# The first SwiGLU of the second layer: its first block of columns in seven half-width products

## The chip, the cores and the metric

The kernel runs on one core of a Trainium2 chip. The metric is the device time of one execution in microseconds (us); the time before is the median of three runs. The traces come from the hardware profiler: one profiled execution, with the start and the length of the instructions on each engine. TensorE (PE in the rows) multiplies and writes PSUM, VectorE (DVE) and ScalarE (ACT) work elementwise, GpSimd (POOL) hardly works here, and SyncE (SP) issues the weight transfers.

## The reference

Two layers work on 512 tokens of width 1024 in float32. Each layer is

```
h = h + 1/2 * SwiGLU_1(RMSNorm(h))      # w_gu 1024 x 5632, w_down 2816 x 1024
h = h + mixer(RMSNorm(h))               # short convolution, attention, gates
h = h + 1/2 * SwiGLU_2(RMSNorm(h))
h = h + sigmoid(RMSNorm(h) @ W_pg) * (p[i] @ W_pp)     # "ple"
swiglu(x) = (silu(g) * u) @ w_down, with g, u the halves of x @ w_gu
```

and a last RMSNorm follows. The change is in the `x @ w_gu` of SwiGLU_1 of the second layer, and in the place of the sum of squares of its RMSNorm.

## The kernel before

**Layout.** Everything is held transposed: `h` is eight tiles of 128 features x 512 tokens. A name in the rows begins with its stage: `a0`, `m0`, `b0`, `e0` are SwiGLU_1, mixer, SwiGLU_2 and ple of the first layer, `a1`, `m1`, `b1`, `e1` those of the second. The stage ahead of `a1` is `e0`.

**Precision.** Each float32 operand is held as two parts, `h` (the rounded value, cast on ScalarE, line 70 for weights and 205 or 208 for activations) and `l` (the rest, subtracted on VectorE, lines 71, 206, 209), and each product is three matmuls, `h*h`, `h*l`, `l*h` (lines 213 to 215, and 451). Weights come by DMA in halves of 128 x 1024 (`st`, 10 buffers) and are split into `wh` and `wl` (4 buffers each).

**Two ways to multiply.** `projs` takes whole columns: 128 output features x 512 tokens. `Sevens` takes a block of 2 x 2 quarters (two halves of the 1024 inputs, two halves of the block's columns) and two halves of the tokens, and makes seven half-width products of 24 matmuls with 256 tokens in place of eight (Strassen's scheme). `Quad` makes the sums of weight quarters on VectorE (lines 142, 147, 150, 153). `Halved` makes the sums of activations: `own(j)` takes row `j` of the lower half of the features (line 393), `other(j)` joins it with row `j+4` (lines 408 to 411) and casts the results `t` and `u`. Product 1 needs rows 0 to 3 of the input alone, product 5 `t` of the lower rows, product 2 rows 4 to 7, products 6, 3, 7 and 4 the joined sums. `step(n, j)` is product `j` of block `n`.

**The norm.** `normed` splits each row of `h` times its gain (`x`), and adds the squares of the rows up one by one in `acc` (line 283). `rms` turns `acc`'s two parts (`ah`, `al`) into sums over the features by two matmuls with ones (`ps`, lines 292 and 293) and takes the reciprocal root `r`, with which results are scaled later.

**What `early` selects.** In `ffn`, `n_whole` is the number of pairs of columns (g and u of 128 features) that are taken whole. It is 4 for the first stage, 2 with `early=2`, and 0 with `early=3`:

```
n_whole = 4 if first else 0 if early > 2 else 2
```

With 2, the first pair is taken whole, then come the two matmuls of the sums, then the second pair, then block 1 in sevens. With 0, block 0 is in sevens as well and the start is

```
            x_ins, sums = ys.other(KD // 2 - 1, xs)

            with tc.issue_after(x_ins):
                step(0, 1)
                step(0, 5)
            r = rms(acc, D, name)
            with tc.issue_after(x_ins):
                step(1, 1)
                step(1, 5)
            order = (2, 6, 3)
```

so that the two matmuls of the sums stand behind two products. `early_rows` makes the rows of `Halved` while the rows of `h` come in: with 2 it makes whole rows 0 and 1 there and the others behind the first columns; with 3 it makes `own` of rows 0 to 3 and `other` of rows 0 to 2, and splits the weights of three products ahead (lines 506 to 514).

**What orders the work.** Instructions are put in order when the program is built, by a scheduler that `issue_after` steers; each engine then has a fixed list. The second SwiGLUs (`b0`, `b1`) use `early=3` already, behind the mixer; `a1` uses 2, behind `e0`. In `e0` each row of `h` is made by `ple_add`: line 963 (VectorE, from the gate's columns), line 965 (sigmoid on ScalarE), lines 969 and 970 on VectorE, where the last is the add to `h`. In the mixer a row of `h` takes one add (line 883).

Of the kernel before, what the change touches and what calls it, by code (L numbers as in the profile page):

```python
# [173 lines left out]
def trunk_kernel(ctx, tc, dims, x, p, positions, gains, rope_c, weights, out):  # L174
# [860 lines left out]
                    dma.dma_start(out=out[row:row + P, kk * 512:(kk + 1) * 512], in_=o)  # L1035

    for l in range(DEPTH):
        ffn(l, "ffn1", f"a{l}", l == 0, rotary if l == 0 else None, 2 if l else 0)
        mixer(l)
        ffn(l, "ffn2", f"b{l}", early=3)  # L1040
        ple(l, l == DEPTH - 1)
# [47 lines left out]
```

## Time and profile before

| | us |
|---|---|
| median of 3 runs (2280.04 to 2280.17) | 2280.16 |
| the profiled execution | 2279.72 |
| its span in the trace | 2277.7 |
| PE busy | 2269.1 |
| DVE busy | 1817.2 |
| ACT busy | 1170.5 |
| mean granted TensorE clock | 0.999 |

A span is the time from the first to the last instruction in the trace. Busy time counts a matmul to its modelled end, so matmuls that follow one another overlap; the distance of two starts tells what one costs in a row. The rows of a timeline give start, length, engine, line and names, and in brackets the idle time of the engine just ahead and what ended it.

### The profile page before, as it was taken

What the parts mean: (1) busy time and instruction counts of PE and PEld (TensorE: products, weight loads), DVE (VectorE), ACT (ScalarE), POOL (GpSimd) and SP (SyncE); (2) the same over time, 40 slices, a digit from 0 to 9 for tenths busy, and PEclk for the clock granted to TensorE, in tenths of its full rate; (3) what the DMA queues carried; (4) which work ended last, traced back from release to release, by engine and by line L of the source; (5) the groups of instructions that cost most, each with busy time, mean ns of one, the idle gap of its engine ahead of it and who ended that gap; (6) DMA issues with size and microseconds to landing.
All of it is one profiled execution on the core that took longest, in us unless ns stands there. A gap on an engine that the chain in (4) does not pass through costs nothing.

```text
span 2277.7 us, 35049 instructions
## 1 busy us (share of the span) xinstructions
PE 2269.1 (100%) x14320; PEld 2063.7 (91%) x14320; DVE 1817.2 (80%) x2540; ACT 1170.5 (51%) x1770; POOL 38.1 (2%) x42
## 2 busy tenths in 40 slices
PE   9999999999999999999999999999999999999998
PEld 8999988899888999998899999888999889999988
DVE  8878778877867988877798887768878689877865
ACT  7444445456745644444664444445567365444455
POOL 0000000000200000000000000000001000000000
PEclk9999999999999999999999999999999999999999
DMA  5333343134121333334223333322331214323321
GB/s 195 113 109 101 104 125 104 55 111 130 47 66 56 110 111 105 102 111 130 83 84 96 109 99 115 121 88 70 112 120 38 74 39 138 111 93 102 112 84 38
DMA packets 63088, 222.77 MB, mean 98 GB/s; under 512 B 7248, under 2 KB 7248, under 8 KB 62928
## 3 DMA queue, kind: packets, MB, share of 16 engines
q1 hardware_dynamic: 62352, 219.76, 30.9%
q8 instruction: 112, 1.84, 0.3%
q10 hardware_dynamic: 576, 0.79, 0.1%
q14 instruction: 48, 0.39, 0.1%
HBM read 218.42 MB, written 2.10 MB: 97 GB/s over the span
## 4 chain that ended last, share of the span: by engine, by line
PE 98%; DVE 1%; ACT 0%; DMA 0%; issue 0%; SPq 0%; ACTq 0%
PE b0pd L213 2%; PE b1pd L213 2%; PE a1pd L213 2%; PE a0pd L213 2%; PE b1pd L214 2%; PE a1pd L214 2%; PE a0pd L214 2%; PE b0pd L214 2%; PE a0pd L215 2%; PE b0pd L215 2%; PE a1pd L215 2%; PE b1pd L215 2%; PE e1gp L213 1%; PE e1gp L215 1%; PE e1gp L214 1%; PE m1mop L213 1%
## 5 line engine op out<-in xcount | busy, mean ns | idle before, releaser
L70 ACT CAST wh<-st 128x1024 fp32r<-128x1024 f32 (+1 forms) x457 | 476.6, 1046 | 564.2 <-issue 64.4
L71 DVE TENSOR_TENSOR wl<-st,wh 128x1024 fp32r<-128x1024 f32 (+1 forms) x458 | 554.7, 1213 | 153.5 <-ACT wh L70 152.9
L70 ACT CAST wh<-s 128x1024 fp32r<-128x1024 f32 x98 | 103.1, 1053 | 132.4 <-DVE s L147 8.9
L71 DVE TENSOR_TENSOR wl<-s,wh 128x1024 fp32r<-128x1024 f32 x98 | 119.4, 1219 | 13.5 <-ACT wh L70 13.4
L150 DVE TENSOR_TENSOR st<-st,s 128x1024 f32<-128x1024 f32 x49 | 60.0, 1224 | 1.2
L147 DVE TENSOR_TENSOR s<-s,st 128x1024 f32<-128x1024 f32 x49 | 59.8, 1220 | 0.2
L142 DVE TENSOR_TENSOR s<-st,st 128x1024 f32<-128x1024 f32 x49 | 59.8, 1220 | 0.1
L153 DVE TENSOR_TENSOR st<-st,st 128x1024 f32<-128x1024 f32 x49 | 59.7, 1219 | 0.1
L559 DVE SCALAR_TENSOR_TENSOR h<-b1pd,h 128x512 f32<-128x512 f32 x40 | 27.6, 689 | 9.0 <-PE b1pd L215 9.0
L559 DVE SCALAR_TENSOR_TENSOR h<-b0pd,h 128x512 f32<-128x512 f32 x40 | 27.6, 689 | 9.0 <-PE b0pd L215 9.0
L559 DVE SCALAR_TENSOR_TENSOR h<-a1pd,h 128x512 f32<-128x512 f32 x40 | 27.6, 689 | 7.6 <-PE a1pd L215 7.5
L559 DVE SCALAR_TENSOR_TENSOR h<-a0pd,h 128x512 f32<-128x512 f32 x40 | 27.5, 688 | 6.4 <-PE a0pd L215 6.3
L107 POOL MEMSET wh<- 128x256 f32 x4 | 1.1, 314 | 1188.9 <-DVE wl L71 1188.9
L296 ACT ACT_TABLE_LOAD x8 | 10.3, 1283 | 0.1
L878 DVE TENSOR_TENSOR m1g<-m1mop,m1g 128x512 f32<-128x512 f32 x8 | 5.5, 690 | 5.9 <-PE m1mop L215 5.9
L878 DVE TENSOR_TENSOR m0g<-m0mop,m0g 128x512 f32<-128x512 f32 x8 | 5.5, 690 | 5.5 <-PE m0mop L215 5.5
L989 ACT ACTIVATE fsq<-h 128x256 f32<-128x256 f32 (+1 forms) x10 | 4.8, 481 | 9.9 <-DVE h L970 9.9
L299 DVE SCALAR_TENSOR_TENSOR e1t<-e1t,e1ms 128x512 f32<-128x512 f32 x1 | 0.7, 696 | 8.5 <-ACT e1ms L298 8.5
L117 DVE TENSOR_TENSOR kl<-st,kh 128x512 fp32r<-128x512 f32 x10 | 6.8, 685 | 0.5 <-ACT kh L116 0.5
L705 DVE TENSOR_TENSOR m1g<-m1cop,m1g 128x512 f32<-128x512 f32 x8 | 5.5, 688 | 2.0 <-PE m1cop L215 2.0
L705 DVE TENSOR_TENSOR m0g<-m0cop,m0g 128x512 f32<-128x512 f32 x8 | 5.5, 687 | 2.0 <-PE m0cop L215 2.0
L676 DVE TENSOR_TENSOR m0z<-m0Vp,m0c 128x512 f32<-128x512 f32 x4 | 2.8, 692 | 5.1 <-PE m0Vp L215 5.1
(11283 smaller groups left out, 8847.7 us busy)
## 6 DMA issues: line engine op xcount, KB each, us to landing
st<-in_weights SPq DMA_DIRECT2D x406, 512.0 KB, 3.6
h<-in_x SPq DMA_DIRECT2D x8, 256.0 KB, 5.4
st<-in_weights SPq DMA_DIRECT2D x7, 256.0 KB, 5.2
out<-fo SPq DMA_DIRECT2D x7, 256.0 KB, 2.3
e0pi<-in_p SPq DMA_DIRECT2D x2, 256.0 KB, 3.7
e1pi<-in_p SPq DMA_DIRECT2D x2, 256.0 KB, 3.8
st<-in_weights ACTq DMA_DIRECT2D x1, 256.0 KB, 3.2
pos_i<-in_positions ACTq DMA_DIRECT2D x1, 256.0 KB, 3.9
```

The lines of the kernel that those rows point to most:

```text
L70: self.nc.scalar.copy(hi[:, w], src[:, w])
L71: last = self.nc.vector.tensor_tensor(lo[:, w], src[:, w], hi[:, w].bitcast(F32), ALU.subtract)
L142: tt(self.s, self.a21, self.a22, ALU.add)
L147: tt(self.s, self.s, self.a11, ALU.subtract)
L150: tt(self.a12, self.a12, self.s, ALU.subtract)
L153: tt(self.a11, self.a11, self.a21, ALU.subtract)
L213: nc.tensor.matmul(ps, wh, vh, start=first, stop=False)
L214: nc.tensor.matmul(ps, wh, vl, start=False, stop=False)
L215: nc.tensor.matmul(ps, wl, vh, start=False, stop=last)
L559: nc.vector.scalar_tensor_tensor(h[m], ps, 0.5, h[m], ALU.mult, ALU.add)
L705: nc.vector.tensor_tensor(gates[m], ps, gates[m], ALU.mult)
L878: nc.vector.tensor_tensor(t, mla_ps[m], t, ALU.mult)
```

## The change

`a1` takes its start in the form that the second SwiGLUs have: `early` is 3 for the second layer's first SwiGLU, which makes `n_whole` 0. The diff is one line:

```
-        ffn(l, "ffn1", f"a{l}", l == 0, rotary if l == 0 else None, 2 if l else 0)
+        ffn(l, "ffn1", f"a{l}", l == 0, rotary if l == 0 else None, 3 if l else 0)
```

Block 0 of `w_gu` (two pairs of columns, 96 matmuls of 512 tokens) becomes seven products (168 matmuls of 256 tokens); the other blocks and `w_down` stay. The order of the instructions shows where the sums stand now.

On VectorE before, from the add that finishes the last row of `h` in `e0` (`h_96`) to the second part of the sum of squares (`a1al`); rows 4 to 6 of the norm were split ahead of these:

```order
L970 TENSOR_TENSOR h_96<-h_96,e0g_11231 128x512
L71 TENSOR_TENSOR wl_11439<-st_11436,wh_11438 128x1024
L283 TENSOR_TENSOR a1acc<-a1acc,a1sq 128x512
L209 SCALAR_TENSOR_TENSOR a1x7l<-h_96,cols,a1x7h 128x512
L283 TENSOR_TENSOR a1acc<-a1acc,a1sq 128x512
L142 TENSOR_TENSOR s<-st_11698,st_11700 128x1024
L206 TENSOR_TENSOR a1al<-a1acc,a1ah 128x512
```

On VectorE of the changed kernel, from the same add, through row 5 of the norm with its joined sums, to the beginning of row 6:

```order
L970 TENSOR_TENSOR h_96<-h_96,e0g_11231 128x512
L209 SCALAR_TENSOR_TENSOR a1x5l<-h_94,cols,a1x5h 128x512
L283 TENSOR_TENSOR a1acc<-a1acc,a1sq 128x512
L409 TENSOR_TENSOR a1t_11258<-a1y_11321,a1x_11257 128x256
L410 TENSOR_TENSOR a1u_11322<-a1t_11258,a1x_11257 128x256
L206 TENSOR_TENSOR a1t1l<-a1t_11258,a1t1h 128x256
L411 TENSOR_TENSOR a1u_11322<-a1y_11321,a1u_11322 128x256
L206 TENSOR_TENSOR a1u1l<-a1u_11322,a1u1h 128x512
L209 SCALAR_TENSOR_TENSOR a1x6l<-h_95,cols,a1x6h 128x512
```

Row 6 takes the same seven instructions, and the list goes on from its last one:

```order
L206 TENSOR_TENSOR a1u2l<-a1u_11341,a1u2h 128x512
L209 SCALAR_TENSOR_TENSOR a1x7l<-h_96,cols,a1x7h 128x512
L283 TENSOR_TENSOR a1acc<-a1acc,a1sq 128x512
L206 TENSOR_TENSOR a1al<-a1acc,a1ah 128x512
L409 TENSOR_TENSOR a1t_11288<-a1y_11393,a1x_11287 128x256
```

So 16 instructions stand between the two rows that enclosed five before. On TensorE of the changed kernel the two matmuls of the sums (`a1ps`) stand between product 5 of block 0 (`a10c`) and product 1 of block 1 (`a11b`):

```order
L451 MATMUL a10c<-a1t3h,wh_11366 128x256
L451 MATMUL a10c<-a1t3l,wh_11366 128x256
L451 MATMUL a10c<-a1t3h,wl_11367 128x256
L292 MATMUL a1ps<-a1ah,ones 128x512
L293 MATMUL a1ps<-a1al,ones 128x512
L451 MATMUL a11b<-a1x0h,wh_11378 128x256
```

That is behind 48 matmuls of 256 tokens; before they stood behind 48 matmuls of 512 tokens.

## Rows read from the trace of the kernel before

**Rows 1.** Part 1 of the page: busy us, share of the span, instructions.

```profile
PE 2269.1 (100%) x14320; PEld 2063.7 (91%) x14320; DVE 1817.2 (80%) x2540; ACT 1170.5 (51%) x1770; POOL 38.1 (2%) x42
```

**Rows 2.** All waits of PE: us in total, times, longest us.

```profile
PE idle L321 <- DVE hpi L251: 1.0, 1, 1.0
PE fss L1001 <- DVE fsq L982: 0.8, 1, 0.8
PE a0pg L231 <- ACT a0x0h L208: 0.2, 1, 0.2
```

**Rows 3.** The chain from 1125 to 1185: start us, us, what.

```profile
1135.03 0.23 PE a1pg L213
...
1145.91 0.24 PE a1ps L292
...
1157.29 2.87 PE a11b L451 x24
1160.16 2.88 PE a11a L451 x24
```

**Rows 4.** The timeline of PE where b1 begins.

```profile
1864.69 0.28 PE L451 MATMUL b10b<-b1x0h,wh 128*128 128x256 f32 x1
...
1867.56 0.28 PE L451 MATMUL b10c<-b1t0h,wh 128*128 128x256 f32 x1
...
1870.44 0.40 PE L292 MATMUL b1ps<-b1ah,ones 128*128 128x512 f32 x1
...
1870.91 0.28 PE L451 MATMUL b11b<-b1x0h,wh 128*128 128x256 f32 x1
```

**Rows 5.** The timeline of DVE where b1 begins.

```profile
1864.89 0.69 DVE L883 TENSOR_TENSOR h<-m1wop,h 128x512 f32<-128x512 f32 x1
1865.50 0.41 DVE L206 TENSOR_TENSOR b1t2l<-b1t,b1t2h 128x256 fp32r<-128x256 f32 x1
1865.83 0.69 DVE L206 TENSOR_TENSOR b1u2l<-b1u,b1u2h 128x512 fp32r<-128x512 f32 x1
1866.44 0.75 DVE L209 SCALAR_TENSOR_TENSOR b1x7l<-h,cols,b1x7h 128x512 fp32r<-128x512 f32 x1
1867.11 0.69 DVE L283 TENSOR_TENSOR b1acc<-b1acc,b1sq 128x512 f32<-128x512 f32 x1
1868.48 0.69 DVE L206 TENSOR_TENSOR b1al<-b1acc,b1ah 128x512 fp32r<-128x512 f32 x1 [0.69 <-ACT b1ah L205]
1869.11 0.43 DVE L409 TENSOR_TENSOR b1t<-b1y,b1x 128x256 f32<-128x256 f32 x1
1869.57 0.42 DVE L410 TENSOR_TENSOR b1u<-b1t,b1x 128x256 f32<-128x256 f32 x1
```

**Rows 6.** The timeline of ACT where b1 begins.

```profile
1867.83 0.62 ACT L205 CAST b1ah<-b1acc 128x512 fp32r<-128x512 f32 x1 [0.90 <-DVE b1acc L283]
...
1871.82 1.28 ACT L296 ACT_TABLE_LOAD   x1
```

**Rows 7.** The timeline of DVE where a1 begins.

```profile
1133.71 0.69 DVE L963 TENSOR_TENSOR e0g<-e0gp,e0r 128x512 f32<-128x512 f32 x1
...
1136.78 0.69 DVE L970 TENSOR_TENSOR h<-h,e0g 128x512 f32<-128x512 f32 x1
1137.38 1.22 DVE L71 TENSOR_TENSOR wl<-st,wh 128x1024 fp32r<-128x1024 f32 x1
1138.52 0.69 DVE L283 TENSOR_TENSOR a1acc<-a1acc,a1sq 128x512 f32<-128x512 f32 x1
...
1141.94 0.69 DVE L206 TENSOR_TENSOR a1al<-a1acc,a1ah 128x512 fp32r<-128x512 f32 x1 [0.33 <-ACT a1ah L205]
```

**Rows 8.** The same stretch of ACT.

```profile
1140.33 1.06 ACT L70 CAST wh<-st 128x1024 fp32r<-128x1024 f32 x1 [1.58 <-issue]
```

**Rows 9.** Stretches at the end: us, busy PE, PEld, DVE, ACT, POOL; then granted clock, DMA.

```profile
2271.00:2272.00 1.00, 0.32 (x3) 0.08 (x2) 0.55 (x4) 0.26 (x1) 0.00 (x0) 1.00 0.00 0
...
2274.00:2275.00 1.00, 0.00 (x0) 0.00 (x0) 0.00 (x0) 0.00 (x0) 0.00 (x0) 0.50 1.00 371
```

## The prediction

> **What bounds the kernel now.** I read the engines' shares first: TensorE is busy 2269.1 of 2277.7 us, VectorE 80%, ScalarE 51% [rows 1]. Then TensorE's waits: there are three in the whole trace, 2.0 us together, two where the kernel begins and one where it ends [rows 2]. So there is no idle time of TensorE around `a1` to win, and none to hide anything in: a matmul saved shortens the time by its own cost, and a wait that the change adds is paid in full, since TensorE has no later wait that could shrink by it.
>
> What one matmul costs is read from the distance of starts. The chain runs through `a1`'s two whole pairs from 1135.03 to 1157.29 [rows 3]: 22.26 us for 98 matmuls of 512 tokens, the 96 of the two pairs and the two of the sums: 0.227 each. A half-width product of 24 matmuls with 256 tokens takes 2.88 [rows 3], 0.120 each: a matmul of half the width costs 53% of a full one.
>
> The third view is the order of the two engines where such a start exists already. In `b1`, product 1 begins at 1864.69, product 5 at 1867.56, the sums at 1870.44 and the next product at 1870.91 [rows 4]: back to back, with no wait. But VectorE finished `b1al` only at 1868.48 + 0.69 = 1869.17 [rows 5]. So in `b1` the sums were ready 1.3 us ahead of their use. `a1` gets that start behind another stage, and the question is whether its sums come in time as well.
>
> **The change part by part.**
>
> *TensorE's work.* Removed: 96 matmuls x 0.227 = 21.8 us. Added: 7 products x 2.88 = 20.2. The gain is 1.6 us, 0.07%. The halves of weights are as many as before, and their transfers too.
>
> *Elementwise work.* Block 0 now needs seven splits of weights in place of four and four sums of quarters, each as long as a split, 1.22 us [rows 7]; VectorE has room for them over the stage, so by themselves I cost them at nothing, as long as they do not stand ahead of something that TensorE waits for. They do, at the start, and that is the rest of this part.
>
> *When TensorE wants the sums.* What precedes `a1` on TensorE is unchanged, so product 1 begins at 1135.03 [rows 3], and `a1ps` is wanted two products on: 1135.03 + 5.76 = 1140.79. Before, it stood 48 full matmuls behind, at 1145.91 [rows 3], and `a1al` was done at 1141.94 + 0.69 = 1142.6 [rows 7], with 3.3 us to spare. It would have been 1.8 us late already for the new place.
>
> *When VectorE delivers them.* The add that makes the last row of `h` stood at 1136.78 [rows 7]. It can't come earlier than the end of `e0`'s matmuls at 1135.03 and two instructions of 0.60 on the way, 1136.3; I take 1136.8 and keep 1136.3 to 1137.8 (one 1.14 us split later). Before, five instructions lay between this add and `a1al`. Now there are 16, in the order shown above: rows 5 and 6 of the norm, each with its joined sums, and row 7. Their cost by distance of starts: line 209 0.67, line 283 0.60 [rows 5, 7], lines 409 and 410 0.46 each, the split of a half row (line 206) 0.33 [rows 5], line 411 followed by the cast of `u` on ScalarE and back. That way there and back is seen between `b1acc` and `b1al`: 1868.48 - 1867.11 = 1.37 behind an add of 0.69, with VectorE idle for 0.69 of it [rows 5], the cast being 0.62 [rows 6]; behind an add of 0.42 it is 0.27 shorter, 1.10. In `b1` other work stood between, here nothing does. Then the split of `u`, 0.60. One row: 0.67 + 0.60 + 0.46 + 0.46 + 0.33 + 1.10 + 0.60 = 4.2 us.
>
> So `a1al` starts at 1136.8 + 0.60 + 2 x 4.2 + 0.67 + 1.37 = 1147.8 and ends at 1148.5. TensorE, which has run the first matmul of the sums on `a1ah` just ahead, waits with the second: 1148.5 - 1140.79 - 0.23 = **7.5 us**. Behind it in TensorE's list stands everything else, product 1 of block 1 first, although its weights are ready by then. With the bounds of `h` this is 7.0 to 8.5.
>
> VectorE keeps its order: at 1141.94 `a1al` had made it wait for 0.33 [rows 7], while the split behind it, whose cast on ScalarE was over at 1140.33 + 1.06 = 1141.39 [rows 8], stayed where it was. The Trainium skill (TensorE: Matmul & The Clock Gate, the table at its head, row on queue depth) states that VectorE and ScalarE take their queues strictly first in, first out; by that rule rows 5 and 6 can't be overtaken, and the trace agrees; if an engine could overtake, the sum would be -1.6.
>
> *What is late next.* TensorE goes on at 1148.75 and wants product 2 of block 0 two products later, at 1154.5. Its weights' second part stands on VectorE behind: row 7's joined sums (0.46 + 0.46 + 0.34), a split of weights (1.14) and of a half row (0.33), which ends at 1151.2 counted from 1148.4; the split of `u`, whose cast stands on ScalarE behind the table load of 1.28 [rows 6] and the first step of the root, so at about 1152.0; then two sums of quarters, 1.14 each, a step of the root, and the split itself, 1.22: 1156.8. The product's third matmul wants it at about 1154.7, so some 2 us are lost; I take **1.8**, between 0 and 2.5. VectorE is busy 80% over the kernel [rows 1], so a lag of 7 us shrinks by a fifth of the time that passes; when block 2's first weights are wanted, some 30 us on, about 1 us of it is left, which I count as **1.1**, between 0 and 2.
>
> *The clock.* At the end of the kernel TensorE's last matmuls lie between 2271 and 2272 at a granted clock of 1.00, and from 2274 on it is 0.50, the 1.2 GHz level [rows 9]: the clock falls soon behind the work. A wait of 7.5 us will very likely do the same, and product 1 of block 1 then runs at half the rate, 2.88 us longer if it stays so for a whole product. How long it stays low no row shows. The first 2.9 us lost in this way cost nothing more, since they take the place of the 1.8 and 1.1 above, which VectorE's list sets and not TensorE; each further product at the low level costs 2.88. I take no more than that, and keep two further ones, 5.8, as the other end. The Trainium skill (the same page, Part 1: The HAM clock gate) states that the throttled clock is the default and activity releases it. By it a stall costs more than its length; the sum by rows has that already up to one product.
>
> *Sum.* -1.6 + 7.5 + 1.8 + 1.1 = +8.8 us. Against the profiled execution, 2279.72, that is 2288.5; the median of the runs stands 0.44 above it, so **2289.0 us**, 0.39% slower.
>
> **The rivals.**
>
> *The sums come in time.* `b1` speaks for it: same start, no wait, and there `b1al` began 3.6 us after the last add to `h` [rows 5]. Against it: there four instructions lay between, of rows 6 and 7 alone, and here the list is 16 long and in sequence. It decides at 1140.3: if `a1al` starts by then, TensorE goes on without a stop and the change gives its -1.6, 2278.6 us. That takes 7.5 us off the walk above.
>
> *The waits half as long.* If VectorE reached rows 5 and 6 well ahead of the add to `h`, the wait would be one row shorter, some 3.3, and nothing late behind it: -1.6 + 3.3 = +1.7, 2281.9. Against it: the list is fixed and the add stands ahead of them.
>
> *The clock stays low.* The wait as forecast, then three products at the low level: 8.8 + 5.8 = +14.6, 2294.8; with two, 2291.9. For it: no row shows the clock rise again once it has fallen [rows 9]. Against it: the products behind the wait follow one another without a gap, but for 2.9 us in all.
>
> **How the numbers follow.** The forecast, with its bounds (7.0 to 8.5 for the first wait, 0 to 4.5 for the others together, -1.6): +5.4 to +11.4, 2285.6 to 2291.6; I give it 0.74. The clock low for two products or more: 0.13. Half as long: 0.05. In time: 0.07. Something that wins more than the counted 1.6: 0.01. A range of 2286.3 to 2292.2 leaves out the low ends, the sums in time and a long low clock. About 0.2%, 4.6 us, is what a measurement of this kernel can tell from no change. Slower: 0.74 and 0.13 and a little of the half case, 0.88. Same: the rest of that, and the sums in time, 0.11. Faster: 0.01.
>
> **What the profile after would show.** Right: among TensorE's waits one at `a1ps` of 7 to 8 us, released by VectorE at `a1al`; `a1al` some 11 us behind the last add to `h` of `e0`; smaller waits or a granted clock of 0.50 in the 10 us behind; seven products of 2.88 in place of 21.8 us, seen in the distance from `a1`'s first matmul to `b1`'s. Wrong: `a1ps` following product 5 without a gap, a wait released by a DMA, or a first product of `a1` that itself starts late because VectorE's longer list held up `e0`.

## The result and the profile after

The changed kernel takes 2290.51 us (median of 6 runs, 2289.66 to 2290.65), the kernel before 2280.16 (6 runs, 2280.04 to 2280.53): a ratio of 1.0045 [1.0034, 1.0055], 10.35 us slower. The forecast was +8.8, 2289.0, with a range of 2286.3 to 2292.2. The profiled execution of the changed kernel took 2290.54 with a span of 2288.4 us.

Part 1 of the page after, beside [rows 1]: TensorE is busy 2.7 us longer, although its work is 1.6 us less.

```profile
PE 2271.8 (99%) x14392; PEld 2069.5 (90%) x14392; DVE 1827.9 (80%) x2556; ACT 1173.2 (51%) x1782; POOL 38.1 (2%) x42
```

All waits of TensorE after, beside [rows 2]: two are new, one at the sums and one at `a12c`, product 5 of block 2.

```profile
PE a1ps L292 <- ACT a1ah L205: 7.3, 1, 7.3
PE idle L321 <- DVE hpi L251: 1.0, 1, 1.0
PE fss L1001 <- DVE fsq L982: 0.8, 1, 0.8
PE a12c L451 <- ACT wh L70: 0.8, 1, 0.8
```

TensorE's timeline after: first matmul of `a1`, the two of the sums, then the first of products 1 and 5 of block 1, of product 2 of block 0 and its third, and the first of block 3.

```profile
1135.67 0.28 PE L451 MATMUL a10b<-a1x0h,wh 128*128 128x256 f32 x1
...
1148.85 0.80 PE L292 MATMUL a1ps<-a1ah,ones 128*128 128x512 f32 x1 [7.26 <-ACT a1ah L205]
1149.57 0.79 PE L293 MATMUL a1ps<-a1al,ones 128*128 128x512 f32 x1
1150.16 0.42 PE L451 MATMUL a11b<-a1x0h,wh 128*128 128x256 f32 x1
...
1154.56 0.28 PE L451 MATMUL a11c<-a1t0h,wh 128*128 128x256 f32 x1
...
1157.44 0.28 PE L451 MATMUL a10a<-a1x4h,wh 128*128 128x256 f32 x1
...
1158.08 0.39 PE L451 MATMUL a10a<-a1x4h,wl 128*128 128x256 f32 x1
...
1202.32 0.28 PE L451 MATMUL a13b<-a1x0h,wh 128*128 128x256 f32 x1
```

The same two ends in TensorE's timeline of the kernel before:

```profile
1134.87 0.39 PE L213 MATMUL a1pg<-a1x0h,wh 128*128 128x512 f32 x1
...
1191.68 0.28 PE L451 MATMUL a13b<-a1x0h,wh 128*128 128x256 f32 x1
```

From the first matmul of `a1` to the first of block 3 is thus 1191.68 - 1134.87 = 56.81 us before and 66.65 after. **The stage is 9.84 longer**, and it adds up from starts alone:

| part of the stage | us |
|---|---|
| 168 half-width matmuls (20.16) for 96 whole ones (21.79) | -1.6 |
| the sums begin at 1148.85, two products (5.76) behind 1135.67 would be 1141.43 | +7.42 |
| the two matmuls of the sums, 1148.85 to 1150.16, before 0.46; the second begins only when `a1al` is done | +0.85 |
| product 1 of block 1, 1150.16 to 1154.56 = 4.40 in place of 2.88 | +1.52 |
| products 2, 6 and 3 of block 0 from 1157.44 | +0.29 |
| three products across block 2's start, 10.03 in place of 8.64 | +1.39 |

Of the 10.82 between the two profiled executions 0.80 more lies ahead of `a1` and 0.2 behind block 3.

VectorE's timeline after, beside [rows 7], from the last add to `h` to the second part of the sums and to the weights of product 2 of block 0:

```profile
1137.57 0.68 DVE L970 TENSOR_TENSOR h<-h,e0g 128x512 f32<-128x512 f32 x1
1138.17 0.74 DVE L209 SCALAR_TENSOR_TENSOR a1x5l<-h,cols,a1x5h 128x512 fp32r<-128x512 f32 x1
...
1142.45 0.75 DVE L209 SCALAR_TENSOR_TENSOR a1x6l<-h,cols,a1x6h 128x512 fp32r<-128x512 f32 x1
...
1146.73 0.75 DVE L209 SCALAR_TENSOR_TENSOR a1x7l<-h,cols,a1x7h 128x512 fp32r<-128x512 f32 x1
1147.40 0.68 DVE L283 TENSOR_TENSOR a1acc<-a1acc,a1sq 128x512 f32<-128x512 f32 x1
1148.83 0.69 DVE L206 TENSOR_TENSOR a1al<-a1acc,a1ah 128x512 fp32r<-128x512 f32 x1 [0.74 <-ACT a1ah L205]
...
1156.81 1.22 DVE L71 TENSOR_TENSOR wl<-st,wh 128x1024 fp32r<-128x1024 f32 x1
```

TensorE waits for the last link of a walk of 11.3 us: the list is followed in order, one row of the norm every 4.28 us, and `a1al` is the seventeenth entry behind the add. The wait is put down to ScalarE (`a1ah`), but ScalarE had only waited for `a1acc` on VectorE:

```profile
1148.18 0.62 ACT L205 CAST a1ah<-a1acc 128x512 fp32r<-128x512 f32 x1 [0.96 <-DVE a1acc L283]
```

Not all of the walk is work of VectorE. In each of rows 5 and 6, and ahead of `a1al`, it stands idle for 0.74 until ScalarE has cast what it needs next, 2.2 us in all. What TensorE waits for is the list that goes to and fro between the two engines.

Stretches after: us, busy PE, PEld, DVE, ACT, POOL, granted clock, DMA.

```profile
1147.00:1149.00 2.00, 0.15 (x1) 0.15 (x1) 1.26 (x3) 1.04 (x3) 0.00 (x0) 0.50 0.00 0
...
1151.00:1153.00 2.00, 2.00 (x12) 2.00 (x11) 1.27 (x2) 1.99 (x3) 0.00 (x0) 0.50 0.02 4
1153.00:1154.00 1.00, 1.00 (x8) 1.00 (x8) 0.80 (x2) 1.00 (x3) 0.00 (x0) 0.68 0.00 0
1154.00:1156.00 2.00, 2.00 (x19) 2.00 (x18) 1.97 (x2) 2.00 (x5) 0.00 (x0) 1.00 0.00 0
```

The clock falls to the 1.2 GHz level (0.50) within the wait and comes back between 1153 and 1154, 4 to 5 us behind the first matmul of the sums: the rows count twelve matmuls in two microseconds at 0.50, nineteen at 1.00.

### The profile page after: what moved, and what is told of

It reads as the page before. It is cut to its first block, busy times and chain, and to the rows that moved or that the text cites. A ratio compares the mean times of both kernels' runs of the same rounds, so it can differ in the third digit from the quotient of the medians.

```text
span 2288.4 us, 35213 instructions
## 1 busy us (share of the span) xinstructions
PE 2271.8 (99%) x14392; PEld 2069.5 (90%) x14392; DVE 1827.9 (80%) x2556; ACT 1173.2 (51%) x1782; POOL 38.1 (2%) x42
## 4 chain that ended last, share of the span: by engine, by line
PE 95%; DVE 3%; ACT 1%; issue 0%; ACTq 0%; DVEq 0%
PE b1pd L213 2%; PE a0pd L213 2%; PE b0pd L213 2%; PE a1pd L213 2%; PE a0pd L214 2%; PE b0pd L214 2%; PE a1pd L214 2%; PE b1pd L214 2%; PE a1pd L215 2%; PE b0pd L215 2%; PE b1pd L215 2%; PE a0pd L215 2%; DVE wl L71 1%; PE e1gp L213 1%; PE e1gp L215 1%; PE e1gp L214 1%
```

## The experiments

The theory: around `a1` VectorE, with the casts of ScalarE that its list waits for, has more to do than time. The sums are only the first place that shows it. The rivals: the place of the sums in TensorE's list is the cause (put them elsewhere and the gain of 1.6 appears), or the fallen clock is. Each kernel was timed against the kernel before on the same chip (2280.20, 2280.37 and 2280.52 in the three groups: the first four, the next four, the last three as they stand below). Since the start and the last store of a program vary by some tenths of a microsecond between executions, I also read the stage as above, `a1`'s first matmul to block 3's first, in each profile:

| kernel | median us | ratio [interval] | stage us | against before |
|---|---|---|---|---|
| before | 2280.16 | | 56.81 | |
| changed | 2290.51 | 1.0045 [1.0034, 1.0055] | 66.65 | +9.84 |
| fillers ahead of the sums | 2291.53 | 1.0049 [1.0037, 1.0062] | 68.22 | +11.41 |
| sums first | 2290.95 | 1.0049 [1.0037, 1.0062] | 67.33 | +10.52 |
| sums behind four products | 2289.46 | 1.0042 [1.0028, 1.0056] | 65.29 | +8.48 |
| no joined sums | 2286.05 | 1.0027 [1.0016, 1.0038] | 62.42 | +5.61 |
| no joined sums, clock kept | 2284.81 | 1.0019 [1.001, 1.0028] | 60.12 | +3.31 |
| no joined sums, early split | 2282.58 | 1.0009 [1.0001, 1.0018] | 57.80 | +0.99 |
| whole pairs in `b1` | 2282.10 | 1.0007 [0.9998, 1.0016] | | |
| two pairs less in `a0` | 2294.47 | 1.0061 [1.0047, 1.0074] | | |
| extra adds in the change | 2292.05 | 1.0051 [1.0037, 1.0065] | 68.36 | +11.55 |
| extra adds in before | 2280.47 | 0.9999 [0.9991, 1.0008] | 56.81 | 0.00 |
| joined sums on GpSimd | 2291.69 | 1.005 [1.0037, 1.0063] | 67.87 | +11.06 |

The intervals of the changed kernel and of most of its variants overlap, so differences of about 1 us between them are not told by the medians; each stage is read from one profiled execution.

**Is it the clock?** Thirty matmuls whose result nobody reads fill the wait:

```
             step(0, 5)
+        if name == "a1":
+            fill = PS(f"{name}fill")
+            for i in range(30):
+                nc.tensor.matmul(fill, xs[0][0][:, :P], xs[0][0], start=True, stop=True)
         r = rms(acc, D, name)
```

> The changed kernel with 30 matmuls of 512 tokens that nobody reads put between product 5 of block 0 and the two of the sums, so that TensorE does not stand still there. Theory (VectorE's list sets the time of the whole stretch): the clock stays at 1.00, but the microseconds saved in product 1 of block 1 come back as waits at product 2 of block 0, about 2 us there instead of none; the time is within 0.6 us of the changed kernel, 2290 to 2291. Rival (the fallen clock is a cost of its own, 1.5 us in product 1 of block 1 and 0.5 in the sums): 2 us faster than the change, about 2288.5.

Measured 2291.53, half a microsecond over the theory's range and far from the rival's: 11.33 over its own before, where the change has 10.35. TensorE's waits in this kernel, then three stretches behind the sums:

```profile
PE a10a L451 <- ACT wh L70: 1.9, 1, 1.9
...
PE a1ps L292 <- ACT a1ah L205: 0.5, 1, 0.5
```

```profile
1149.00:1156.00 7.00, 5.93 (x49) 5.68 (x47) 5.95 (x10) 6.97 (x13) 0.00 (x0) 1.00 0.00 1
```

```profile
1158.00:1160.00 2.00, 1.85 (x12) 1.65 (x12) 2.00 (x3) 0.00 (x0) 0.00 (x0) 0.77 0.35 143
1160.00:1162.00 2.00, 2.00 (x11) 2.00 (x11) 0.63 (x1) 1.34 (x2) 0.00 (x0) 0.50 0.16 16
```

Until product 2 of block 0 (`a10a`) the clock stays at 1.00 and nothing is gained: a wait of 1.9 stands there, which the change does not have, and the product begins 21.57 behind `a1`'s first matmul (1156.82 - 1135.25) against 21.77 in the change. Up to this point the fallen clock only filled time in which TensorE would have waited for weights.

Behind that wait the clock falls after all. From 1159 to 1162.6 the starts within product 2 stand up to 0.21 apart in place of 0.12, which is 1.5 us longer. So the fillers moved the low clock and did not do away with it, and the run does not tell what the low level costs later in the stage. Three things make this stage 1.57 longer than the change's: the 1.5; the order on VectorE, where the last step of the root (line 300) stands ahead of product 2's split here, at 1156.53, and behind it in the change, at 1157.94, so that the split begins 0.75 later counted from `a1`'s first matmul (1157.14 - 1135.25 against 1156.81 - 1135.67); and, the other way, 0.7 less across block 2's start (9.31 in place of 10.03).

**Is it the place of the sums?** First the other way round: VectorE does the norm's rows and the sums before any joined sum (`self_last` collects the last instruction of a split).

```
-                elif j < early:
+                elif j < (0 if name == "a1" else early):
                     ys.other(j, xs)
...
         if n_whole == 0:
+            if name == "a1":
+                with tc.issue_after(self_last[-1].ins):
+                    for j in range(0, KD // 2 - 1):
+                        ys.other(j, xs)
```

> The changed kernel with all joined rows (lines 408 to 411 and their splits) queued behind the sums of squares on VectorE, so that the sums are ready some 11 us earlier. Theory (VectorE is behind with its work as a whole, the sums are only the first to show it): no wait at the sums, but one of 6 to 8 us at product 5 of block 1, whose weights now stand behind the joined rows; 2287.5 to 2291 in all. Rival (the sums of squares that stand in front of TensorE's list are the cause): the 7.4 us of wait are gone, 2282 to 2283.

Measured 2290.95. TensorE's longest wait in this kernel, then the timelines of VectorE and of ScalarE:

```profile
PE a11c L453 <- ACT wh L70: 7.7, 1, 7.7
```

```profile
1141.01 0.69 DVE L208 TENSOR_TENSOR a1al<-a1acc,a1ah 128x512 fp32r<-128x512 f32 x1 [0.69 <-ACT a1ah L207]
...
1153.09 1.22 DVE L71 TENSOR_TENSOR wl<-s,wh 128x1024 fp32r<-128x1024 f32 x1
```

```profile
1151.70 1.03 ACT L70 CAST wh<-s 128x1024 fp32r<-128x1024 f32 x1
```

`a1al` comes 7.8 us earlier, the sums are in time but for 0.2 at the second matmul, and the wait is as long as ever, one product on: the weights of product 5 of block 1 (`a11c`) now stand behind the joined sums, their cast in ScalarE's list and their second part in VectorE's.

Then TensorE's side: products 1 and 5 of block 1 go ahead of the sums.

```
-            r = rms(acc, D, name)
-            with tc.issue_after(x_ins):
-                step(1, 1)
-                step(1, 5)
+            if name == "a1":
+                with tc.issue_after(x_ins):
+                    step(1, 1)
+                    step(1, 5)
+                r = rms(acc, D, name)
+            else:
...
```

> The changed kernel with the two matmuls of the sums placed behind four products in place of two. Theory (VectorE behind as a whole): TensorE runs product 1 of block 1 in the old wait, then waits 5 to 7 us with product 5 of block 1 for its weights, which stand behind the sums on VectorE; 1 to 1.5 us faster than the change, 2289 to 2289.5. Rival (place of the sums): the wait shrinks by the two products, 5.8 us, to 1.6; 2284 to 2285.

Measured 2289.46, 9.26 over its own before and so 1.1 less than the change. TensorE's longest wait in this kernel:

```profile
PE a11c L451 <- ACT wh L70: 5.9, 1, 5.9
```

Again the wait moves to `a11c` and stays. With neither place of the sums does the gain of 1.6 appear; the rival that lays the loss on them falls.

**Is it VectorE's work?** Here all joined sums of `a1` are left out, and with them their casts on ScalarE; the products that need them read rows of the norm.

```
             x_ins = nc.scalar.mul(y, h[k], gain(self.nm, self.l, k))
+            if self.name == "a1":
+                for p_, v, at in ((2, xs[k], left), (3, xs[k], right), (7, xs[j], right), (6, xs[k], left), (4, xs[j], right)):
+                    self.ys[p_].append(tuple(w[:, at] for w in v))
+                return x_ins.ins, self_last[-1].ins
```

> The changed kernel without the joined sums of a1: lines 409 to 411 and the splits of their results are left out, and products 3, 4, 6 and 7 read rows of the norm in their place. TensorE's work is the same, VectorE has some 11 us less of it at the start. Theory (VectorE behind): no wait at the sums; one of about 3 us is left at product 5 of block 1, whose weights ScalarE's list casts late; 2281.5 to 2284.5. Rival (something else holds TensorE, transfers or the place of the sums): above 2288.

Measured 2286.05: 4.5 less than the change, but 1.5 over the range that I gave. TensorE's waits, then stretches of this kernel:

```profile
PE a11c L457 <- ACT wh L70: 2.8, 1, 2.8
```

```profile
1150.00:1152.00 2.00, 2.00 (x12) 2.00 (x11) 2.00 (x3) 0.00 (x0) 0.00 (x0) 0.50 0.00 0
1152.00:1154.00 2.00, 2.00 (x11) 2.00 (x11) 0.36 (x1) 0.00 (x0) 0.00 (x0) 0.50 0.09 12
1154.00:1155.00 1.00, 1.00 (x9) 1.00 (x8) 0.00 (x0) 0.89 (x2) 0.00 (x0) 0.87 0.89 352
```

A wait of 2.8 stays at `a11c`. It is not VectorE's: the weights' cast stands in ScalarE's list behind the table load, the steps of the root and a copy, from 1142.39 to 1146.26, and VectorE itself is idle for 2.5 us there. The clock falls behind the wait and stays at 0.50 until 1154, while VectorE is hardly busy from 1152 on (0.36 of 2.00), so that nothing covers it. Two kernels part the wait and the clock. The one keeps the clock with eleven matmuls ahead of product 5 of block 1:

```
             step(1, 1)
+            if name == "a1":
+                fill = PS(f"{name}fill")
+                for i in range(11):
+                    nc.tensor.matmul(fill, xs[0][0][:, :P], xs[0][0], start=True, stop=True)
             step(1, 5)
```

> The run without the joined sums (left out as there), with 11 matmuls of 512 tokens that nobody reads ahead of product 5 of block 1, in place of most of its 2.8 us wait. Theory (a fallen clock costs time where VectorE is not behind; in the changed kernel its cost was covered): the clock stays at 1.00, and the 3.4 us that products took longer at the low level are saved: 2282.3 to 2283.5. Rival (the clock's cost is covered here too): within 0.7 us of the run without the fillers, 2285.4 to 2286.7.

Measured 2284.81, between the two ranges. Against their own befores the two kernels differ by 1.4 (5.85 and 4.44), their stages by 2.30; the profiled execution without fillers, 2287.14, was the longest of its seven. So the low clock costs 1.4 to 2.3 here, less than the 3.4 expected. TensorE's waits in this kernel, then a stretch with the clock:

```profile
PE a10a L457 <- ACT wh L70: 0.4, 1, 0.4
...
PE a11c L457 <- ACT wh L70: 0.3, 1, 0.3
```

```profile
1150.00:1153.00 3.00, 3.00 (x27) 3.00 (x26) 2.45 (x3) 0.97 (x2) 0.00 (x0) 1.00 0.00 0
```

The other takes the wait away: the weights of product 5 of block 1 are split ahead of the first product.

```
             with tc.issue_after(x_ins):
+                if name == "a1":
+                    sevens.split(1, 5)
                 step(0, 1)
```

> The run without the joined sums (they are left out as there), with the weights of product 5 of block 1 split ahead of the first products, so that the 2.8 us wait and the fallen clock behind it go as well. Theory (VectorE's and ScalarE's lists alone hold TensorE back): 1 to 1.5 us of waits are left against 1.6 us won by the seven products: 2279.5 to 2282. Rival (the seven products at this place cost something that no list explains): 2284 or more.

Measured 2282.58, 0.6 above the range. TensorE's waits in this kernel:

```profile
PE a10b L457 <- ACT wh L70: 0.9, 1, 0.9
...
PE a10a L457 <- ACT wh L70: 0.4, 1, 0.4
```

Without the joined sums, and with one split moved ahead, the stage is 0.99 longer than before in place of 9.84. So nine tenths of the loss go with the elementwise work of the joined sums, on VectorE and ScalarE (4.23), and with the place of one split and the low clock behind its wait (4.62). The starts give what is left: product 2 of block 0 and the two behind it lose 1.9 us, the three products across block 2's start 0.7, against the 1.6 won. The change with this split moved ahead and the joined sums kept was not run. The profiled executions of the three kernels without joined sums also have a longer last store, 6.5 us from the first output instruction to the end of the span, against 5.7 before; that 0.8 has nothing to do with `a1`, and whether their medians have it too is not shown.

**Is the saving itself real?** The kernel before, with `b1` put back to whole pairs:

```
-        ffn(l, "ffn2", f"b{l}", early=3)
+        ffn(l, "ffn2", f"b{l}", early=3 if l == 0 else 2)
```

> The kernel before, with the second SwiGLU of the second layer (b1) in the other form: two whole pairs first, then block 1. It measures the gain of the seven products by themselves, where the sums were in time. Theory (no wait in either form, 21.8 against 20.2 us of matmuls): 1.6 us slower than before, 2281.8. Rival (whole pairs give VectorE room that is worth something here as well): not slower than before, 2280.2 or less.

Measured 2282.10, 1.73 slower, with an interval that just takes in no change; the traces carry the reading: from `b1`'s first matmul to the first output instruction the traces differ by 1.58 (1865.76 to 2274.68, before 1864.69 to 2272.03). So the products win their 1.6 where the elementwise engines keep up. And the same trade where the kernel has most whole pairs, `a0`:

```
-        n_whole = 4 if first else 0 if early > 2 else 2
+        n_whole = 0 if early > 2 else 2
```

> The kernel before, with two whole pairs in place of four in the very first SwiGLU (a0), so that its block 1 goes in seven products. The same trade at another place where VectorE is busy nearly all the time. Theory (whole pairs are what lets VectorE keep up with TensorE): 6 to 12 us of waits in the first 70 us against 1.6 won, 2285 to 2291. Rival (the trouble is special to the sums of squares behind e0, which stay in their place here): 1.6 us faster, 2278.6.

Measured 2294.47, slower as expected and by more, 14.1 us and 3.5 over the range. TensorE's two longest waits in this kernel, then ScalarE's and VectorE's timelines and a stretch of it:

```profile
PE a01c L451 <- ACT a0t3h L205: 3.5, 1, 3.5
PE a02b L451 <- DVE wl L71: 2.0, 1, 2.0
```

```profile
43.94 1.05 ACT L70 CAST wh<-st 128x1024 fp32r<-128x1024 f32 x1 [1.88 <-PE a02b L451]
```

```profile
45.02 1.23 DVE L71 TENSOR_TENSOR wl<-st,wh 128x1024 fp32r<-128x1024 f32 x1 [2.09 <-ACT wh L70]
```

```profile
40.00:45.00 5.00, 4.68 (x28) 4.48 (x27) 2.86 (x5) 1.68 (x3) 0.00 (x0) 0.71 0.20 83
```

Again weights and casts come late; with the shorter waits it is 8.9 us in `a0`. But this run shows the loss at a second place and not the same cause alone: VectorE is busy for only 2.86 of 5 us from 40 to 45, since its split waits for a cast, and ScalarE begins that cast only behind a matmul of TensorE (43.94). The granted clock falls to 0.71 there and to 0.84 from 50 to 60, which the forecast left out.

**Does VectorE's time count one to one?** Four adds of 128 x 512 in rows 6 and 7 of `a1`'s norm, once in the change and once in the kernel before:

```
+            if name == "a1" and k >= KD - 2:
+                scratch = rp.tile([P, S], F32, tag="w", name=f"dose{k}")
+                nc.vector.tensor_tensor(scratch, h[k], h[k], ALU.add)
+                nc.vector.tensor_tensor(sq.acc, sq.acc, scratch, ALU.add)
```

> The changed kernel with four more adds of 0.60 us on VectorE ahead of the last part of the sums (h + h of rows 6 and 7, added into the sums of squares, which changes what they hold). Two fall partly into gaps of VectorE's list of 0.36 and 0.12 us, so the sums come about 1.8 us later. Theory (VectorE's list up to the sums is what TensorE waits for): the wait at the sums grows from 7.3 to 8.8 to 9.3 us and the time by 1.5 to 2.0, 2292.0 to 2292.5. Rival (the wait is set elsewhere, and VectorE has room): as the change, 2290.5.

> The kernel before with the same four adds (the sums of squares are changed in the same way). There the sums had 3.3 us to spare. Theory: no wait of TensorE, the time of before within 0.3 us, 2280.0 to 2280.6. Rival (VectorE's work has a price wherever it stands): 1.5 to 2.4 us slower, 2281.8 to 2282.7.

Measured 2292.05 and 2280.47. The first is 11.53 over its own before, 1.2 more than the change; the second is not changed from before. TensorE's wait in the first:

```profile
PE a1ps L292 <- ACT a1ah L205: 8.9, 1, 8.9
```

VectorE and TensorE in the second:

```profile
1144.67 0.69 DVE L206 TENSOR_TENSOR a1al<-a1acc,a1ah 128x512 fp32r<-128x512 f32 x1
```

```profile
1146.49 0.40 PE L292 MATMUL a1ps<-a1ah,ones 128*128 128x512 f32 x1
```

In the change the wait is 1.6 longer and the stage 1.71, close to the 1.8 that the gaps do not take in. In the kernel before `a1al` begins 2.0 later, counted from `a1`'s first matmul (1135.61 here), and still ends 1.1 us ahead of the two matmuls; the stage is 56.81 to the hundredth. So the list up to `a1al` sets the wait in the change, and has room in the kernel before.

**Can another engine take it?** The sums of `own` and `other` go to GpSimd in `a1`:

```
...
+            eng = nc.gpsimd if self.name == "a1" else nc.vector
-            nc.vector.tensor_tensor(t[:, right], y[:, right], x[:, right], ALU.subtract)
+            eng.tensor_tensor(t[:, right], y[:, right], x[:, right], ALU.subtract)
...
```

> The changed kernel with the sums of activations of a1 (lines 393 and 409 to 411) on GpSimd, which is idle there: 6.4 us less for VectorE. Theory, if GpSimd takes some 0.9 us for each of the 16 (it took 0.6 us for 128 columns and 1.25 for 384 in the trace of before): the wait at the sums shrinks to 4 to 5 us and one of 3 to 4 appears at product 2 of block 0, whose weights wait for a chain that now passes through a slower engine; 2287 to 2290. Rival (moving the work frees VectorE, and the sums come in time by as much): 6 us faster than the change, 2284 to 2285.

Measured 2291.69, 11.17 over its own before: 0.8 more than the change (1.2 by the stage), where I had expected it faster. TensorE's waits, VectorE's and GpSimd's timelines of this kernel:

```profile
PE a1ps L292 <- ACT a1ah L205: 5.6, 1, 5.6
PE a10a L453 <- ACT wh L70: 2.4, 1, 2.4
```

```profile
1136.36 0.68 DVE L283 TENSOR_TENSOR a1acc<-a1acc,a1sq 128x512 f32<-128x512 f32 x1
...
1141.91 1.22 DVE L283 TENSOR_TENSOR a1acc<-a1acc,a1sq 128x512 f32<-128x512 f32 x1
```

```profile
1141.84 0.74 POOL L411 TENSOR_TENSOR a1t<-a1y,a1x 128x256 f32<-128x256 f32 x1 [2.49 <-ACT a1y L409]
```

The wait at the sums is 5.6, where I had 4 to 5, and one of 2.4 stands at product 2 of block 0, where I had 3 to 4; the change has 7.3 and none. The 12 joined sums and 4 others took 0.9 us on GpSimd in the mean, as I had counted; what I had left out is that they slow VectorE. An add on VectorE that begins 0.07 behind one on GpSimd takes 1.22 in place of 0.68, about as long as if it began when the other ended. The Trainium skill (SBUF — State Buffer, section Who interferes with whom) states that a VectorE instruction with two inputs in SBUF contends with a GpSimd instruction that reads SBUF, and that the order of issue decides which one blocks; these rows agree.

## Why the prediction was right, and where it was off

The time lies in the range and the mechanism is the one forecast; the sum was 1.0 short of the stage's +9.84 and 1.5 short of the medians.

**The gain of 1.6.** Right: -1.6 from the same durations after, and +1.58 where `b1` gives it up.

**The first wait, 7.5.** Right in place, and one link off in the releaser. I had TensorE run the first matmul of the sums at once and wait with the second, for `a1al`. It waited 7.26 with the first already, for ScalarE's `a1ah`, and then with the second until `a1al` was done: 0.72 from start to start in place of 0.23. The second began 7.9 late. The list is longer than forecast by 0.3: `a1al` stands 11.26 behind the last add to `h` (I had 11.0), since a row takes 4.28 in place of 4.2 and the way to ScalarE and back 1.43 in place of 1.37. The add itself came 1.90 behind `a1`'s first matmul where I had 1.77: I took that first matmul from the chain, whose row stands 0.16 behind the timeline's (1135.03 against 1134.87). At the low clock the next product then began 0.59 behind the second matmul in place of 0.23, so that TensorE left the sums 8.27 late.

**Product 2 of block 0, 1.8.** The price stands, but its place moved. The split was forecast to end at 1156.8; it ended at 1158.03, of which 0.6 is the later start of `a1` against 1135.03. With the fillers the wait for this product's weights is 1.9. In the change there is none, since the fallen clock holds product 1 of block 1 for 1.52; the first matmul that needs the split begins at 1158.08, 0.05 behind its end.

**The lag later, 1.1.** Mis-sized: 0.29 and 1.39. Together the later terms are 3.20 in place of 2.9, half of it as matmuls at the low clock in place of waits, as the forecast allowed.

**The elementwise work, nothing by itself.** The added splits and sums are 8.5 us; VectorE's busy time rises by 10.7 (1817.2 to 1827.9), so even its size was taken too small. No run prices it by itself.

**The clock.** It falls and comes back within one product, so the rival in which it stays low falls; no row before showed how long it would stay, so to that extent the forecast was lucky. That its first part costs nothing more, because the weights of product 2 are late anyway, is shown by the kernel with the fillers, in which product 2 begins only 0.2 us earlier. Where the elementwise engines are not late it does cost, 1.4 to 2.3 us, by the two kernels without joined sums.

**What was wrong beside the sum** is a rival's price: "if `a1al` starts by then, TensorE goes on without a stop and the change gives its -1.6". In the kernel with the sums first, `a1al` began at 1141.01 with `a1` at 1135.56, 0.15 behind the need, and the kernel was as slow as the change: 7.7 us of wait at `a11c`. An early `a1al` alone is thus not enough when the joined sums that it passed still have to be made. I had treated the wait at the sums as the fault and the lag behind it as a rest of 2.9. By the two waits, 7.3 at the sums and 7.7 at `a11c`, the lists of VectorE and ScalarE are, as an estimate, some 8 us behind what TensorE is going to need, and TensorE stops at whichever instruction first needs the end of them. The whole pairs ask VectorE for four splits (4.9 us) in 21.8 us of TensorE's time; seven products ask for seven splits and four sums (11 x 1.22 = 13.4 us) in 20.2. So in the kernel before the pairs are the time in which VectorE catches up, and the adds that cost 1.6 in the change cost nothing there.

**Open.** The 0.8 us ahead of `a1` in the profiled executions: 0.61 of it at the kernel's first matmul, which stands at 6.18 after and 5.57 before and varies likewise between the other kernels. What the fallen clock costs in the later part of the stage. How much of the loss the one split moved ahead would take away with the joined sums in place. No kernel here beats the one before.

## What to carry to other kernels

A product scheme that saves matmuls pays in elementwise work, so it paid here only where the elementwise engines had caught up: the same trade won 1.6 us behind the mixer and lost 10 behind the gated stage. Before pricing a wait, follow the other engines' lists past the instruction that is waited for, to the next ones that TensorE needs: if these are late too, moving the first only moves the wait. And when a run is meant to keep the clock up, read the clock to the end of the stage, since a wait that moves can take the low clock with it. Matmuls that ask little of the other engines are worth keeping where those are behind.

## What the runs showed of the hardware

The granted clock fell to 0.50 behind a wait of only 2.8 us (kernel without joined sums) and stayed there from 1148 to 1154, with TensorE busy for 1.80 of the first 2 us and for all of the rest; in the change, behind a wait of 7.3, it was back between 1153 and 1154, with TensorE at work since 1148.85. In the kernel with fillers it fell behind a wait of 1.9 and a short one. What the fallen clock costs depends on the engines behind it: nothing as long as the next product's weights were late (product 2 at 21.57 and 21.77), 1.4 to 2.3 us where they were not. A GpSimd sum of half a row took 0.73 to 1.60 us, against 0.42 on VectorE, and slowed an add beside it from 0.68 to 1.22.
